# A fourth seven-product pair in each FFN of a two-layer encoder, with outputs added in a seeded PSUM bank

## The chip, the cores and the metric

The kernel runs on one core of a Trainium2 chip. The metric is the device time of one execution in microseconds (us), the median of several runs. The core has TensorE (matrix products; PE in the profile, with its weight loads as PEld), VectorE (DVE), ScalarE (ACT), GpSimd (POOL) and SyncE (SP, which here issues the loads of weights from memory). Each engine works through its own queue in order and waits on semaphores for what the others make. Matrix products are added up in PSUM, in banks of 128 x 512 fp32 values; everything else stands in SBUF.

## The reference

A two-layer encoder over 256 tokens of width 1024, in fp32. Each layer has two branches (gated linear attention and grouped-query attention), two gates that merge them, a SwiGLU feed-forward network (FFN) and an embedding that is added at the end. The change lies in the FFN and in gate B.

```python
D_MODEL, SEQ, DEPTH = 1024, 256, 2
FFN_HIDDEN = -(-8 * D_MODEL // (3 * 256)) * 256      # 2816 = 11 blocks of 256

def hybrid_layer(h, ...):
    u = rms_norm(h, g_mix_pre)
    (..., gate_a, gate_b) = jnp.split(u @ w_in, offsets, axis=-1)
    ...
    mixed = jax.nn.sigmoid(gate_a) * branch_a + jax.nn.sigmoid(gate_b) * branch_b
    h = h + rms_norm(mixed @ w_out, g_mix_post)

    gate, up = jnp.split(rms_norm(h, g_ffn_pre) @ w_ffn_in, 2, axis=-1)
    h = h + rms_norm((jax.nn.silu(gate) * up) @ w_ffn_out, g_ffn_post)

    e = p_i @ w_ple_proj
    return h + rms_norm(jax.nn.sigmoid(h @ w_ple_gate) * e, g_ple_post)
```

## The kernel before

**Products.** The 256 tokens are two halves of 128. Every fp32 operand is kept as a high and a low part in a reduced format (fp32r), and a product is three passes: high by high, low by high, high by low. Weights come in *units* of 128 x 2048 values, 1 MB, which is four slices of 128 rows by 512 columns. One unit against one half of the tokens is 12 matmuls of 128 x 512 (`passes`, L112): first the eight that need the unit's high part `wh`, then the four that need its low part `wl`. Against both halves a unit is 24 matmuls.

**The stream of weights** (`Stream`, L245). A plan, written out once for all layers, lists the units in order. SyncE loads a unit into one of two `raw` tiles. `split` (L130) then makes its parts, each in two pieces of 1024 columns: ScalarE copies the high part (L132), VectorE subtracts it from the source for the low part (L133; `vsub`, L128, is the line that the profile shows). The parts go to one of four `wh`/`wl` pairs of the pool `wp`. The stream runs ahead of TensorE as far as these tiles allow.

**Pairs of blocks with seven products** (`seven`, L608). Two column blocks of 512 by two halves of the contraction form a 2 x 2 matrix of units b11, b12, b21, b22; the tokens' two halves by the two halves of the contraction form another, a11 to a22. Instead of eight products of 12 matmuls, seven are made of sums of the a's and sums of the b's. The token sums are made by VectorE and split once per FFN (`sums`, L583; the four *forms*). The sums of units are made by `Stream.step` (L320), one call per product, with in-place adds of 2048 columns on VectorE. In its code the pair's four loads are x (b11), z (b12), y (b22) and q (b21): x and z are loaded into one of the `wp` pairs that the stream lends for this (`lent`, L275; the next pair's x and z may not be loaded before `lend` is set in the last step), y into a `big` tile, and q into a `raw` tile. The seven outputs are combined to four output blocks by 512-column operations on VectorE (L615 and `vsub`), with copies of single products from PSUM to SBUF by ScalarE (L635, L638, L642). For a pair of FFN blocks, the output blocks are gate and up of one token half each, and `gated` (L1438) makes SiLU(gate) on ScalarE and multiplies by up on VectorE.

**The FFN's order.** The hidden width is 11 blocks of 256. Blocks 0 and 1 come first, by halves. Then a string written by hand (L40) sets the order: `u` is a plain unit (24 matmuls; two make a block), a digit is that product of the current pair (12 matmuls), `o` is one step of the output projection (24 matmuls with a unit of `w_ffn_out`), `p` a load of a gain. Before each output step, the hidden values it needs are turned by TensorE transposes and split (hidden parts, tile `hid`, via `turned`, L1382). Blocks 4, 5 and 10 are plain, and 2-3, 6-7 and 8-9 are pairs.

```python
FFN = "uu12u34u5u67" "uo12o34o5o67" "poo12o345o67"
PLAIN, PAIRS = (4, 5, 10), (2, 6, 8)
OUT = (0, 1, 2, 3, 4, 5, 10, 6, 7, 8, 9)
```

Gate B is one more such pair, with plain units between its products (`GATES`, L47: `uuu1u2m34m5m67m`). The order of instructions within each engine's queue comes from a scheduler that works by priorities over this program order, so that an operation can stand earlier in a queue than its line suggests.

## Time and profile before

| what | before |
|---|---|
| time, median of 3 runs (range) | 924.27 us (923.92 to 924.66) |
| profiled execution, span from its first to its last instruction | 922.9 us |
| mean granted TensorE clock | 0.998 |
| TensorE matmuls busy | 912.2 us, 99% of the span |
| VectorE busy | 786.1 us, 85% |
| ScalarE busy | 578.5 us, 63% |
| bytes read from memory | 169.50 MB, 187 GB/s with what is written |

Busy times of neighbouring instructions of an engine overlap a little, so what one instruction costs its queue is read from the start of one to the start of the next. The profile names tiles without their numbers: `acc_0ffnin` is any accumulator of layer 0's FFN input, `wl_1ffnin` any low part in layer 1's. L numbers are lines of the kernel; helpers such as `vsub` (L128) and `vmul` (L125) give one line to many operations, which are told apart by their tiles.

### The profile page before, as it was taken

The page shows a single profiled execution, that of the slowest core. Times are in us where ns is not written, and L with a number is a line of the kernel's source. Part 1 is how long each engine was busy: PE and PEld are TensorE (multiplying, and loading weights), DVE is VectorE, ACT ScalarE, POOL GpSimd, SP SyncE. Part 2 cuts the span into 40 slices and gives each one's busy share as a digit, 9 for nine tenths or more (in the row PEclk, how much of TensorE's full clock was granted, in tenths as well). Part 3 has the DMA queues.
Part 4 walks back from the last instruction along what each step waited for, and adds up shares of the span by engine and source line. Part 5 has one row for each costly group of instructions (what it writes and reads, how often), then busy time and mean ns, then how long its engine had stood idle before and what let it go on. Part 6 is the DMA issues. An engine that isn't in the chain of part 4 may idle for free.

```text
span 922.9 us, 12406 instructions
## 1 busy us (share of the span) xinstructions
PE 912.2 (99%) x4668; PEld 776.2 (84%) x4668; DVE 786.1 (85%) x1002; ACT 578.5 (63%) x954; POOL 83.8 (9%) x147
## 2 busy tenths in 40 slices
PE   9999999999999999999999999999999999999996
PEld 6898888888888888888899988888888888888885
DVE  6898989987579998999779789798875799989884
ACT  4669676664567656566676677765644766565563
POOL 3400211300000000000114001100001000000000
PEclk9999999999999999999999999999999999999999
DMA  7463455656286565647576424454573756545361
GB/s 260 144 230 134 148 173 188 201 193 232 90 277 222 178 233 168 265 128 268 188 256 220 153 92 137 137 191 174 195 260 104 268 177 204 223 177 217 126 239 45
DMA packets 88679, 173.44 MB, mean 188 GB/s; under 512 B 3422, under 2 KB 26470, under 8 KB 88108
## 3 DMA queue, kind: packets, MB, share of 16 engines
q1 hardware_dynamic: 88460, 172.40, 54.0%
q8 instruction: 36, 0.59, 0.3%
q10 hardware_dynamic: 160, 0.27, 0.1%
q14 instruction: 23, 0.19, 0.1%
HBM read 169.50 MB, written 3.15 MB: 187 GB/s over the span
## 4 chain that ended last, share of the span: by engine, by line
PE 94%; DVE 2%; ACT 1%; DMA 1%; issue 1%; POOL 0%; POOLq 0%; DVEq 0%; ACTq 0%; SPq 0%
PE acc_0ffnin L120 12%; PE acc_1ffnin L120 11%; PE acc_1gate L120 7%; PE acc_0gate L120 7%; PE acc_0ffnin L104 7%; PE acc_1ffnin L104 7%; PE acc_1rq L120 3%; PE acc_0gqk L120 2%; PE acc_0wout L120 2%; PE acc_1gqk L120 2%; PE acc_1ple L120 2%; PE acc_0ple L120 2%; PE acc_0gg L120 2%; PE acc_1gg L120 2%; PE acc_0v L120 2%; PE acc_1merge L120 2%
## 5 line engine op out<-in xcount | busy, mean ns | idle before, releaser
L104 PE MATMUL acc_0ffnin<-wh_0ffnin,big_0ffnin 128*128 128x512 f32 x176 | 56.9, 393 | 0.0
L104 PE MATMUL acc_1ffnin<-wh_1ffnin,big_1ffnin 128*128 128x512 f32 x176 | 56.8, 392 | 0.0
L132 ACT CAST wh_1ffnin<-raw_1ffnin 128x1024 fp32r<-128x1024 f32 x38 | 38.5, 1049 | 27.3 <-DMA raw_1ffnin<-in_w_ffn_out_dram 8.7
L132 ACT CAST wh_0ffnin<-raw_0ffnin 128x1024 fp32r<-128x1024 f32 x38 | 38.4, 1048 | 23.8 <-PE acc_0ffnin L120 7.8
L128 DVE TENSOR_TENSOR wl_1ffnin<-raw_1ffnin,wh_1ffnin 128x1024 fp32r<-128x1024 f32 x38 | 45.0, 1221 | 8.9 <-ACT wh_1ffnin L132 8.9
L128 DVE TENSOR_TENSOR wl_0ffnin<-raw_0ffnin,wh_0ffnin 128x1024 fp32r<-128x1024 f32 x38 | 44.8, 1220 | 7.1 <-ACT wh_0ffnin L132 7.0
L120 PE MATMUL acc_1ffnin<-wh_1ffnin,big_1wout 128*128 128x512 f32 x168 | 42.5, 393 | 0.0
L120 PE MATMUL acc_0ffnin<-wh_0ffnin,big_0wout 128*128 128x512 f32 x168 | 42.5, 393 | 0.0
L104 PEld LDWEIGHTS acc_0ffnin<-wh_0ffnin,big_0ffnin 128*128 128x128 f32 x176 | 33.0, 188 | 7.1 <-DVE big_0ffnin L128 0.5
L104 PEld LDWEIGHTS acc_1ffnin<-wh_1ffnin,big_1ffnin 128*128 128x128 f32 x176 | 33.1, 188 | 6.7
L128 DVE TENSOR_TENSOR wl_1ffnin<-lent_1ffnin,wh_1ffnin 128x1024 fp32r<-128x1024 f32 x30 | 35.8, 1218 | 1.7 <-ACT wh_1ffnin L132 1.7
L128 DVE TENSOR_TENSOR wl_0ffnin<-lent_0ffnin,wh_0ffnin 128x1024 fp32r<-128x1024 f32 x30 | 35.8, 1216 | 1.7 <-ACT wh_0ffnin L132 1.7
L120 PEld LDWEIGHTS acc_1ffnin<-wh_1ffnin,big_1wout 128*128 128x128 f32 x168 | 31.1, 188 | 6.2
L120 PEld LDWEIGHTS acc_0ffnin<-wh_0ffnin,big_0wout 128*128 128x128 f32 x168 | 31.1, 188 | 6.2
L132 ACT CAST wh_1ffnin<-lent_1ffnin 128x1024 fp32r<-128x1024 f32 x30 | 30.7, 1053 | 7.1 <-PE acc_1ffnin L104 3.9
L132 ACT CAST wh_0ffnin<-lent_0ffnin 128x1024 fp32r<-128x1024 f32 x30 | 30.7, 1054 | 6.7 <-PE acc_0ffnin L104 3.9
L104 PE MATMUL acc_0ffnin<-wl_0ffnin,big_0ffnin 128*128 128x512 f32 x88 | 34.3, 389 | 0.0
L104 PE MATMUL acc_1ffnin<-wl_1ffnin,big_1ffnin 128*128 128x512 f32 x88 | 34.3, 389 | 0.0
L128 DVE TENSOR_TENSOR wl_1gate<-raw_1gate,wh_1gate 128x1024 fp32r<-128x1024 f32 x20 | 23.6, 1219 | 5.4 <-ACT wh_1gate L132 5.3
L128 DVE TENSOR_TENSOR wl_0gate<-raw_0gate,wh_0gate 128x1024 fp32r<-128x1024 f32 x20 | 23.7, 1226 | 4.8 <-ACT wh_0gate L132 4.8
L132 ACT CAST wh_0gate<-raw_0gate 128x1024 fp32r<-128x1024 f32 x20 | 20.0, 1048 | 11.7 <-DMA raw_0gate<-in_w_o_attn_dram 5.6
L132 ACT CAST wh_1gate<-raw_1gate 128x1024 fp32r<-128x1024 f32 x20 | 20.0, 1049 | 11.5 <-DMA raw_1gate<-in_w_o_attn_dram 5.5
(695 smaller groups left out, 2691.8 us busy)
## 6 DMA issues: line engine op xcount, KB each, us to landing
raw_0ffnin<-in_w_ffn_out_dram SPq DMA_DIRECT2D x11, 1024.0 KB, 6.6
raw_1ffnin<-in_w_ffn_out_dram SPq DMA_DIRECT2D x11, 1024.0 KB, 5.1
lent_0ffnin<-in_w_ffn_in_dram SPq DMA_DIRECT2D x6, 1024.0 KB, 7.4
lent_1ffnin<-in_w_ffn_in_dram SPq DMA_DIRECT2D x6, 1024.0 KB, 8.3
raw_0v<-in_w_in_dram SPq DMA_DIRECT2D x4, 1024.0 KB, 4.9
raw_0gate<-in_w_o_gla_dram SPq DMA_DIRECT2D x4, 1024.0 KB, 4.9
raw_0gate<-in_w_o_attn_dram SPq DMA_DIRECT2D x4, 1024.0 KB, 5.1
raw_0wout<-in_w_ffn_in_dram SPq DMA_DIRECT2D x8, 512.0 KB, 4.9
```

What stands on the lines that cost most here:

```text
L104: return nc.tensor.matmul(o, lhsT, rhs, start=start, stop=stop)
L120: nc.tensor.matmul(o, x, y, start=start and n == 0, stop=stop and n == len(seq) - 1, **kw)
L128: nc.vector.tensor_tensor(out=out, in0=in0, in1=in1, op=ALU.subtract)
L132: nc.scalar.copy(hi, src)
```

## The change

- Blocks 4 and 5 become a fourth pair (4-5), block 10 stays plain. The string is new: products 1 to 4 of a pair follow one another, then an output step, then 5, 6 and 7.
- `step` makes the unit sums in another order: product 2 now uses x+z, product 3 the unit q, product 4 the sum with y, product 5 y, product 6 the sum with q, product 7 the sum z+y. q is loaded before product 3 and not before 5; lending is allowed, and loading started, in step 6 and no longer in 7.
- One PSUM bank is held for a whole stage (`bank`: the first accumulator of the stage). VectorE seeds it with p5 − p1 after product 2; product 4 adds onto it; ScalarE copies it out to u4; product 5 adds onto it, ScalarE copies it out as c12 and writes u4 back into it; product 7 adds onto that, and it serves as the last output block. Two 512-column VectorE operations per pair are left beside the SiLU multiplies, where there were five.
- Low parts of the pairs' units (gate B's too), of the output units and of plain block 10 are made by one VectorE subtract of 2048 columns. High parts are still copied in two pieces of 1024.

```diff
-FFN = "uu12u34u5u67" "uo12o34o5o67" "poo12o345o67"
-PLAIN, PAIRS = (4, 5, 10), (2, 6, 8)
-OUT = (0, 1, 2, 3, 4, 5, 10, 6, 7, 8, 9)
+FFN = "uu1234o567" "oo1234o567" "po1234o567" "o1234o567"
+PLAIN, PAIRS = (10,), (2, 4, 6, 8)
+OUT = (0, 1, 10, 2, 3, 4, 5, 6, 7, 8, 9)
...
-                    if n == 5:
+                    if n == 3:
                         self.loads.append(q)
...
         def made(self, x):
-            for piece in self.put(x):
-                split(*piece)
+            pieces = self.put(x)
+            if not x.wide:
+                for piece in pieces:
+                    split(*piece)
+                return
+            for hi, _, src in pieces:
+                nc.scalar.copy(hi, src)
+            wh, wl = (t[:, : x.n] for t in self.ready[-1])
+            vsub(wl, x.raw[:, : x.n], wh.bitcast(F32))
 
         def step(self, n, x, y, z, q):
-            c = slice(0, 2048)
+            def add(to, b):
+                c = slice(0, 2048)
+                nc.vector.tensor_tensor(out=to.raw[:, c], in0=to.raw[:, c], in1=b.raw[:, c], op=ALU.add)
+
             if n == 1:
                 self.made(x)
-                nc.vector.tensor_tensor(out=x.raw[:, c], in0=x.raw[:, c], in1=z.raw[:, c], op=ALU.add)
+                add(x, z)
             elif n == 2:
+                self.made(x)
+                add(x, y)
+            elif n == 3:
+                self.made(q)
+            elif n == 4:
+                self.made(x)
+                add(x, q)
+                self.load()
+            elif n == 5:
                 self.made(y)
-                nc.vector.tensor_tensor(out=z.raw[:, c], in0=z.raw[:, c], in1=y.raw[:, c], op=ALU.add)
-            elif n == 3:
-                self.made(x)
-                nc.vector.tensor_tensor(out=x.raw[:, c], in0=x.raw[:, c], in1=y.raw[:, c], op=ALU.add)
-            elif n == 4:
-                self.made(z)
-            elif n == 5:
-                self.made(x)
-                nc.vector.tensor_tensor(out=x.raw[:, c], in0=x.raw[:, c], in1=q.raw[:, c], op=ALU.add)
+                add(z, y)
             elif n == 6:
-                self.made(q)
-            else:
-                self.load()
                 self.made(x)
                 self.held -= 1
                 self.lend = True
+                self.start()
+            else:
+                self.made(z)
...
-    def seven(sp, forms, gated):
+    def seven(sp, forms, gated, bank):
...
+        (p1, u4), (c12, c21) = (halves(mid()) for _ in range(2))
+        c11, p5 = acc(), acc()
+
+        def upper():
+            nc.scalar.copy(c12, bank[0])
+            nc.scalar.copy(bank[0], u4)
+            gated(0, c11, c12)
 
         def last():
-            vsub(v, p5, c22)
-            gated(1, v, c22)
+            vsub(c21, p1, bank[0])
+            gated(1, c21, bank[0])
 
         times(c11, quad(0, 0), True, lambda: nc.scalar.copy(p1, c11))
         yield
         task.need()
-        product(0, lambda: nc.scalar.copy(p3, o[0]))
+        times(p5, form(1), True, lambda: vsub(bank[0], p5, p1))
         yield
-        times(p5, form(1), True, lambda: vsub(v, p5, p1))
+        times(c11, quad(0, 1), False)
         yield
-        product(2, lambda: nc.scalar.copy(p7, o[0]))
+        times(bank[0], form(3), False, lambda: nc.scalar.copy(u4, bank[0]))
         yield
-        product(3, both)
+        times(bank[0], form(0), False, upper)
         yield
-        times(c11, quad(0, 1), False, lambda: gated(0, c11, c12))
+        times(p5, quad(1, 1), False, lambda: nc.scalar.copy(p1, p5))
         yield
-        times(p5, quad(1, 1), False, last)
+        times(bank[0], form(2), False, last)
         yield
...
+                if not hf + b:
+                    bank = [o]
```

28 lines of the change are left out of this document (13 added, 15 removed).

## The prediction, made before the changed kernel ran

> **What bounds the kernel now.** I read the page first: the sums by engine and the chain that ended last.
>
> ```profile
> span 922.9 us, 12406 instructions
> PE 912.2 (99%) x4668; PEld 776.2 (84%) x4668; DVE 786.1 (85%) x1002; ACT 578.5 (63%) x954; POOL 83.8 (9%) x147
> PEclk9999999999999999999999999999999999999999
> PE 94%; DVE 2%; ACT 1%; DMA 1%; issue 1%; POOL 0%; POOLq 0%; DVEq 0%; ACTq 0%; SPq 0%
> ```
>
> TensorE makes the end: 94% of the chain. Its waits, in the view of waits for that engine, are all of the list:
>
> ```profile
> PE warm L104 <- DVE keep L142: 1.6, 1, 1.6
> PE acc_0rq L120 <- ACT big_start L142: 0.6, 1, 0.6
> PE aux_start L142 <- DVE mid_start L142: 0.4, 1, 0.4
> PE aux_1at L104 <- DVE mid_1at L128: 0.2, 1, 0.2
> ```
>
> That is 2.8 us, and none of it in the FFN. So a matmul less is worth its whole price, as long as the other engines keep up; and any microsecond that they fall behind is added at full price too. VectorE's 85% over the span hides where it works. The windows of the pair stretch in layer 0 (columns: stretch, length, then busy time of PE, PEld, DVE, ACT, POOL, the granted clock, DMA share, GB/s) show it:
>
> ```profile
> 283.00:296.00 13.00, 13.00 (x61) 10.71 (x60) 13.00 (x14) 8.38 (x14) 0.00 (x0) 1.00 0.64 210
> 296.00:320.00 24.00, 24.00 (x110) 19.87 (x109) 22.66 (x22) 15.95 (x20) 0.00 (x0) 1.00 0.39 133
> 320.00:343.00 23.00, 23.00 (x107) 19.07 (x106) 22.32 (x24) 12.28 (x16) 0.95 (x1) 1.00 0.75 274
> 343.00:369.00 26.00, 26.00 (x120) 21.53 (x120) 22.83 (x20) 17.61 (x21) 0.00 (x0) 1.00 0.45 147
> 369.00:391.00 22.00, 22.00 (x101) 18.21 (x100) 20.53 (x20) 10.52 (x13) 0.00 (x0) 1.00 0.74 280
> 391.00:421.00 30.00, 30.00 (x136) 24.85 (x135) 27.56 (x26) 20.78 (x24) 0.00 (x0) 1.00 0.43 132
> ```
>
> From 283 to 421 us TensorE is busy all 138.0 us and VectorE 128.9: 93%, and 13.00 of 13.00 in the first stretch. This is the engine to which the change gives more work. (ScalarE has 85.5 of 138.)
>
> **The change part by part.** Prices first, start to start, since busy times of neighbours overlap.
>
> ```profile
> 282.26 1.88 DVE L128 TENSOR_TENSOR mid_0ffnin<-mid_0wout,mid_0ffnin 128x512 fp32r<-128x512 f32 x3
> 284.06 1.22 DVE L128 TENSOR_TENSOR wl_0ffnin<-raw_0emb,wh_0ffnin 128x1024 fp32r<-128x1024 f32 x1
> ...
> 285.53 0.41 DVE L125 TENSOR_TENSOR t_0ffnin<-acc_0ffnin,t_0ffnin 128x256 f32<-128x256 f32 x1
> 285.87 1.21 DVE L128 TENSOR_TENSOR wl_0ffnin<-raw_0emb,wh_0ffnin 128x1024 fp32r<-128x1024 f32 x1
> 287.00 2.35 DVE L128 TENSOR_TENSOR wl_0ffnin<-lent_0ffnin,wh_0ffnin 128x1024 fp32r<-128x1024 f32 x2
> 289.27 0.68 DVE L128 TENSOR_TENSOR mid_0ffnin<-t_0ffnin,mid_0ffnin 128x512 fp32r<-128x512 f32 x1
> 289.87 2.28 DVE L324 TENSOR_TENSOR lent_0ffnin<-lent_0ffnin,lent_0ffnin 128x2048 f32<-128x2048 f32 x1
> 292.07 0.41 DVE L128 TENSOR_TENSOR big_0ffnin<-aux_0ffnin,big_0ffnin 128x256 fp32r<-128x256 f32 x1
> ```
>
> VectorE: 512 columns (284.06 − 282.26)/3 = 0.60; 256 columns 285.87 − 285.53 = 0.34; a low part in two 1024 pieces 289.27 − 287.00 = 2.27; an add of 2048 columns 292.07 − 289.87 = 2.20. A low part 2048 wide isn't in this trace: I give it the add's 2.20, same width and sources; bounds 2.20 and the 2.28 that the row has as busy.
>
> ```profile
> 284.19 5.46 PE acc_0ffnin L120 x24
> 289.65 0.22 PE aux_0ffnin L439 x2
> ```
>
> TensorE, from the chain of waits: a matmul 5.46/24 = 0.2275, a transpose 0.11.
>
> *Removed.* Two blocks cost 96 matmuls as plain units, 84 as a pair: 12 fewer per FFN, 24 in all, the very count of that row: −5.5 us.
>
> *Moved to VectorE.* Per FFN the fourth pair brings four adds of 2048 columns, 8.8 us, and three units more to split (7 against 4), 6.6. Off go 1.8 per pair for the output sums (five 512 operations become two), some 0.07 per unit for wide splits, and the plain blocks' multiplies. What decides is where this falls. In the new order of products, 1 2 3 4 run with nothing between them, and at most an output step between 7 and the next 1. VectorE works its queue in order, and the bank's seed (`bank = p5 − p1`) is new: product 4 adds to the bank, so TensorE waits there. By the changed program's queue, ahead of the seed stand the low parts of 1, 2, 3, 4, the adds x+z, z+y, x+y, x+q, and the small operations between.
>
> *First pair.* Here VectorE has no slack and TensorE's time of product 1 is as before:
>
> ```profile
> 295.18 1.98 PE L120 MATMUL acc_0ffnin<-wh_0ffnin,big_0wout 128*128 128x512 f32 x8
> ...
> 300.62 1.98 PE L120 MATMUL acc_0ffnin<-wh_0ffnin,big_0wout 128*128 128x512 f32 x8
> 302.43 1.07 PE L120 MATMUL acc_0ffnin<-wl_0ffnin,big_0wout 128*128 128x512 f32 x4
> 303.35 0.60 PE L1424 MATMUL aux_0ffnin<-ident,t_0ffnin 128*128 128x128 f32 x4
> ```
>
> Before, plain block 4's second unit had its low part done at 287.0. One wide subtract can't be cut around the SiLU multiply between its halves, 0.5 later: 287.5. Then low part 1 2.2, a form 0.6, hidden part 0.34, x+z 2.2 (292.8), multiply 0.34, z+y 2.2, low 2 2.2 (297.6), multiply 0.34, x+y 2.2, low 3 2.2 (302.3, just in time for 302.43), low 4 2.2, hidden 0.6, x+q 2.2, seed 0.6: 307.9. TensorE ends product 3 at 303.35, then four transposes (0.44) and four high matmuls of the output step that stand ahead of product 4 (0.91): ready at 304.7. **Stall 3.2 us.**
>
> *Between pairs* the same loop closes on itself. The next pair's x lands in the buffer whose last reader is low part 6, so its load can't be issued before that. From one seed: x+q, output step, 5, 6, four operations of 2048 columns, 8.8 us; then the load, whose price is in these rows of SyncE's queue and ScalarE:
>
> ```profile
> 373.87 0.92 SPq L294 DMA_DIRECT2D lent_0ffnin<-in_w_ffn_in_dram  x2
> 379.07 2.01 ACT L132 CAST wh_0ffnin<-lent_0ffnin 128x1024 fp32r<-128x1024 f32 x2 [0.90 <-DMA lent_0ffnin<-in_w_ffn_in_dram]
> ```
>
> ScalarE waited for x, so it landed 379.07 − 373.87 = 5.2 us after issue. Here VectorE does low 7, low of an output step and a multiply (5.0) and then idles. ScalarE's two copies of 512 columns stand ahead of the cast, 1.2 by the row
>
> ```profile
> 298.20 0.58 ACT L635 COPY mid_0ffnin<-acc_0ffnin 128x512 f32<-128x512 f32 x1
> ```
>
> (a copy into PSUM is not in the trace: 0.5 to VectorE's 0.7), the cast 2.0 as above: 8.8 + 5.2 + 1.2 + 2.0 = 17.2. Then seven operations of 2048 columns (low 1, 2, 3, 4, x+z, z+y, x+y), 15.4, and five small ones of 0.6, 3.0, to the next seed: 35.6, with 0.2 for hand-overs (0.2 is the longest late wait of TensorE above) 35.8. TensorE's work in that loop, with one output step (24 matmuls) beside seven products (84) and a second output step (24): 132 × 0.2275 + 8 × 0.11 = 30.9. **Stall 4.9 us**, before pairs 3 and 4. Between pairs 1 and 2 stand two output steps, then TensorE has 24 matmuls more, 36.4 against 35.8: no stall (up to 0.6 to spare, lost if VectorE's operations cost 2.28).
>
> Landing is bounded by 4.9 below (other 1 MB loads) and 6.6 above:
>
> ```profile
> raw_0ffnin<-in_w_ffn_out_dram SPq DMA_DIRECT2D x11, 1024.0 KB, 6.6
> raw_0v<-in_w_in_dram SPq DMA_DIRECT2D x4, 1024.0 KB, 4.9
> ```
>
> *At nothing:* wide low parts in the gate and output stages and the gate pair's bank (units lie between its products, as now, which give VectorE some 5 us each; without them it would stall like the FFN); 12 casts and 26 copies more on ScalarE, in its 38% idle, except the 1.2 above; q's load moved earlier in SyncE's queue, behind raw loads that are waiting anyway. z's load waits for TensorE and is needed one add after x, no later than the x chain.
>
> *Sum:* per layer 3.2 + 0 + 4.9 + 4.9 = 13.0, twice 26.0, less 5.5: +20.5. On the span 922.9 that is 943.4; the median lies 1.4 above that span (924.27), so **945 us**, some 2.2% slower. Its own range: with the first pair's stall hidden after all, 945 − 6.4 = 938.6; with operations at 2.28 (11 on each loop's path, 0.9) and landing 6.6 (1.4) in four loops, and 0.7 (9 operations) for each first pair, 945 + 10.6 = 955.6.
>
> **The rivals.** (a) *The saving lands whole.* For it: VectorE's sums rise by little over the whole span, and TensorE never waited for it so far. Against it: from product 1 to product 4 TensorE needs 9.5 us (295.18 to 304.7), and VectorE's queue from low 1 to the seed 18.4; no lead covers that where VectorE already ran 13.00 of 13.00. 924.3 − 5.5 = 918.8. Chance 0.09. (b) *VectorE's own work is the only limit*: if x lands and is cast before VectorE has come to it, the loop is 8.8 + 5.0 + 18.4 = 32.2 and the later stalls 1.3 each: 2 × (3.2 + 1.3 + 1.3) = 11.6 − 5.5, +6.1: 930.4. Against it: it needs the load issued 3.4 us ahead of low part 6, and that buffer is in use. If still more is hidden it comes near no change. Chance 0.08, of which 0.03 for no change. (c) *A restart costs more.* The first matmuls of the kernel:
>
> ```profile
> 1.65 3.17 PE L104 MATMUL warm<-keep 128*128 128x512 bf16 x7 [1.65 <-DVE keep L142]
> ```
>
> Seven in 3.17 us, 0.45 each, twice the 0.2275 of later, though the clock row shows a full clock there. If TensorE starts so again after each stall, 3.17 us at half pace lose 7 × 0.2275 = 1.6 us; six stalls, 9.6: 955. Against it: the clock row shows no such stretch, but no wait here after the start is over 0.6 us. Chance 0.07. The Trainium skill, "TensorE: Matmul & The Clock Gate", Part 1: The HAM clock gate, has a rule for it: the array falls to half rate after an idle window of about 3.4 us and is back after as much sustained work. By that rule stalls of 4.9 us would always pay and those of 3.2 mostly not, four of six, which would give some 951; the start agrees with it (0.45 against 0.2275), the rest no row here shows.
>
> **How the numbers follow.** Forecast 0.76, (a) 0.09, (b) 0.08, (c) 0.07. About 0.2%, 1.8 us, is what this kernel's measurement can tell from no change. Faster: (a), 0.09. Same: 0.03, of (b). Slower: 0.05 + 0.76 + 0.07 = 0.88. The range reaches from 928, below (b)'s 930.4, to 958, above the forecast's 955.6 and most of (c); (a) and the rest of (b) are left out, with some of (c).
>
> **What would show it.** TensorE's waits, now 2.8 us, would be some 29, with the bank's seed on VectorE as releaser ahead of product 4 in the first, third and fourth pair of both FFNs, about 3, 5 and 5 us, and nothing in the second. 24 fewer 512-column matmuls; wide low parts near 2.28 busy. VectorE without a gap from block 10 to the first seed, with one gap of about 3 us in later pairs while x lands, ended by ScalarE's cast. The step on the load is wrong if VectorE has no such gap, the seed step if TensorE waits for low parts or for nothing. A time under 926 with no new waits is (a); matmuls at 0.45 after a stall are (c).

## The result and the profile after

The changed kernel takes 964.0 us (median of 4 runs, 962.94 to 964.17) against 924.38 of the kernel before on the same chip (923.92 to 924.66): a ratio of 1.0422, 95% interval 1.0409 to 1.0434. That is 39.6 us slower. The forecast had the sign and the places of the waits in the FFN, but 20.7 us, and its range ended at 958. One execution of a version below, order_wide, took 5203.52 us, far above its other three, and its ratio leaves it out.

First the page of the changed kernel: its span, the sums by engine, the granted clock in 40 slices, and the chain that ended last.

```profile
span 962.3 us, 12308 instructions
PE 921.2 (96%) x4644; PEld 776.8 (81%) x4644; DVE 798.1 (83%) x902; ACT 600.7 (62%) x988; POOL 80.0 (8%) x147
PEclk9999999999999999999899999999999999999999
PE 76%; DVE 15%; ACT 4%; issue 3%; DMA 1%; POOL 0%; SPq 0%; POOLq 0%; DVEq 0%; ACTq 0%
```

The matmuls fell by the 24 of the change (4668 to 4644), but TensorE's share of the last chain fell from 94% to 76%: VectorE and ScalarE now stand in it. One slice of the clock row shows an 8, where before all were 9. The view of TensorE's waits (line waited for, releaser, total, times, longest), first rows:

```profile
PE aux_0ffnout L457 <- DVE h L555: 7.4, 1, 7.4
PE acc_0ffnin L120 <- DVE wl_0ffnin L128: 6.1, 2, 3.0
PE acc_1ffnin L120 <- DVE wl_1ffnin L128: 6.1, 2, 3.1
PE acc_1ffnin L120 <- DVE acc_1ffnin L128: 4.2, 2, 3.4
PE acc_0ffnin L120 <- DVE acc_0ffnin L128: 3.4, 1, 3.4
```

Per FFN there is one wait of 3.4 us for the bank's seed (pair 1; in layer 1 a short one besides) and two of 3.0 for a low part (pairs 3 and 4). The largest wait of all, 7.4, is at the end of layer 0 and in no line of the forecast.

**Pair 1.** TensorE's timeline, then VectorE's (start, duration, instruction, idle time before and its releaser):

```profile
304.11 1.08 PE L104 MATMUL acc_0ffnin<-wh_0ffnin,big_0ffnin 128*128 128x512 f32 x4
308.63 3.48 PE L120 MATMUL acc_0ffnin<-wh_0ffnin,mid_0ffnin 128*128 128x512 f32 x8 [3.43 <-DVE acc_0ffnin L128]
```

```profile
305.68 2.28 DVE L337 TENSOR_TENSOR lent_0ffnin<-lent_0ffnin,raw_0ffnin 128x2048 f32<-128x2048 f32 x1
307.88 0.69 DVE L128 TENSOR_TENSOR acc_0ffnin<-acc_0ffnin,mid_0ffnin 128x512 f32<-128x512 f32 x1
```

The seed starts at 307.88 and x+q, 2.20 ahead of it, as the forecast's queue had it. New is what follows the wait: eight matmuls in 3.48 us, 0.43 each, where 0.2275 is usual. Product 4 of this pair costs some 1.5 us more.

**From pair to pair.** Product 4 starts at 308.63, 346.47, 383.18 and 419.17 in layer 0:

```profile
346.47 2.01 PE L120 MATMUL acc_0ffnin<-wh_0ffnin,mid_0ffnin 128*128 128x512 f32 x8
...
379.72 1.95 PE L120 MATMUL acc_0ffnin<-wl_0ffnin,big_0wout 128*128 128x512 f32 x4 [3.05 <-DVE wl_0ffnin L128]
...
419.17 2.88 PE L120 MATMUL acc_0ffnin<-wh_0ffnin,mid_0ffnin 128*128 128x512 f32 x8
```

The loops are 37.84, 36.71 and 35.99. TensorE's own work in them, by the forecast's count, is 36.4, 30.9 and 30.9, so 1.4, 5.8 and 5.1 are lost. VectorE's timeline in the second of these loops, then ScalarE's, TensorE's and SyncE's rows beside its gap:

```profile
345.65 0.69 DVE L128 TENSOR_TENSOR acc_0ffnin<-acc_0ffnin,mid_0ffnin 128x512 f32<-128x512 f32 x1
...
358.11 2.29 DVE L128 TENSOR_TENSOR wl_0ffnin<-lent_0ffnin,wh_0ffnin 128x2048 fp32r<-128x2048 f32 x1 [2.97 <-PE acc_0ffnin L120]
360.31 0.69 DVE L125 TENSOR_TENSOR t_0ffnin<-mid_0ffnin,t_0ffnin 128x512 f32<-128x512 f32 x1
360.92 2.29 DVE L128 TENSOR_TENSOR wl_0ffnin<-raw_0ffnin,wh_0ffnin 128x2048 fp32r<-128x2048 f32 x1
363.32 2.29 DVE L128 TENSOR_TENSOR wl_0ffnin<-lent_0ffnin,wh_0ffnin 128x2048 fp32r<-128x2048 f32 x1
...
381.78 0.69 DVE L128 TENSOR_TENSOR acc_0ffnin<-acc_0ffnin,mid_0ffnin 128x512 f32<-128x512 f32 x1
```

```profile
356.01 2.00 ACT L330 CAST wh_0ffnin<-lent_0ffnin 128x1024 fp32r<-128x1024 f32 x2 [4.89 <-PE acc_0ffnin L104]
...
361.29 2.00 ACT L330 CAST wh_0ffnin<-lent_0ffnin 128x1024 fp32r<-128x1024 f32 x2
```

```profile
355.58 0.39 PE L104 MATMUL acc_0ffnin<-wh_0ffnin,big_0ffnin 128*128 128x512 f32 x1
...
356.94 1.07 PE L120 MATMUL acc_0ffnin<-wl_0ffnin,mid_0ffnin 128*128 128x512 f32 x4
```

```profile
355.16 0.98 SPq L298 DMA_DIRECT2D lent_0ffnin<-in_w_ffn_in_dram  x2
```

VectorE's operations of 2048 columns are 2.28 busy and 2.20 from start to start, as forecast. Its gap of 2.97 us is there too, but two units earlier than forecast: ahead of low part 7 (358.11), not ahead of the next pair's low part 1 (363.32). ScalarE's cast for product 7 (356.01) had waited 4.89 us for TensorE at line 104, which is the output step behind product 4: its last matmul ends at 355.97, and that frees a weight buffer. VectorE's own row names another releaser, TensorE at line 120: these are product 5's low matmuls, which end at 358.01, just when the cast does. So product 7 seems to wait for two buffers, one for its high part, that the output step frees, and one for its low part, that product 5 frees behind it. In pair 1 the second alone ends the gap: there the cast is done at 319.61, product 5's low matmuls end at 320.29, and low part 7 starts at 320.38. The cast of the next pair's x at 361.29 shows no wait; ScalarE comes to it from other work 6.1 us after SyncE issued the load.

**The end of layer 0.** Where the next layer's decay weights are loaded and split, and the FFN's post norm; before (SyncE, VectorE):

```profile
396.12 0.31 SPq L717 DMA_DIRECT2D mid_0ffnin<-in_w_alpha_up_dram  x1
```

```profile
419.84 1.22 DVE L128 TENSOR_TENSOR mid_0ffnin<-mid_0ffnin,mid_0ffnin 17x1024 fp32r<-17x1024 f32 x1
...
431.70 1.28 DVE L125 TENSOR_TENSOR mid_0ffnout<-acc_0ffnin,mid_0ffnin 128x512 f32<-128x512 f32 x2
```

and after (SyncE, GpSimd, VectorE, TensorE):

```profile
447.55 0.50 SPq L729 DMA_DIRECT2D mid_0ffnin<-in_w_alpha_up_dram  x1
```

```profile
449.36 0.57 POOL L511 TENSOR_TENSOR rstd_0ffnout<-rstd_0ffnout,neghalf 128x1 f32<-128x1 f32 x1
```

```profile
455.29 2.36 DVE L128 TENSOR_TENSOR wl_0ffnout<-raw_0ffnin,wh_0ffnout 128x1024 fp32r<-128x1024 f32 x2 [2.79 <-ACT wh_0ffnout L132]
457.68 1.22 DVE L128 TENSOR_TENSOR mid_0ffnin<-mid_0ffnin,mid_0ffnin 17x1024 fp32r<-17x1024 f32 x1
458.91 1.29 DVE L125 TENSOR_TENSOR mid_0ffnout<-acc_0ffnin,mid_0ffnin 128x512 f32<-128x512 f32 x2
```

```profile
460.91 1.97 PE L457 MATMUL aux_0ffnout<-ident,h 128*128 128x128 f32 x8 [7.42 <-DVE h L555]
```

Before, the last of the three small loads of weights left SyncE's queue at 396.12, and the split (17 x 1024) ran 12 us ahead of the post norm. Now that load leaves at 447.55, behind raw loads which wait for buffers; the split runs at 457.68, and the post norm of the first half, whose statistics were ready at 449.9, stands behind it and behind low parts that wait for their casts. TensorE waits 7.4 us for `h` and then runs at half rate again (eight small transposes in 1.97 us). The windows view has a granted clock of 0.91 there (columns as in the prediction):

```profile
430.00:470.00 40.00, 32.58 (x145) 26.69 (x144) 29.68 (x29) 22.33 (x32) 1.73 (x4) 0.91 0.65 226
```

**The ledger.** For every matmul of a stage I took the time from its start to the next start, less the median of matmuls of its size, and summed. The FFN of layer 0 has 17.4 us of such excess more than before, that of layer 1 17.6, the end of layer 0 10.0. With the 24 matmuls less, 17.4 + 17.6 + 10.0 − 5.5 = 39.5; the spans differ by 962.3 − 922.9 = 39.4. Layer 0's 17.4 is 3.6 at pair 1's seed, 1.4, 5.8 and 5.1 in the loops, and 1.5 behind pair 4.

### The profile page after: what moved, and what is told of

Read it like the earlier page. It is cut to its first block, busy times and chain, and to the rows that moved or that the text cites. A ratio compares the mean times of both kernels' runs of the same rounds, so it can differ in the third digit from the quotient of the medians.

```text
span 962.3 us, 12308 instructions
## 1 busy us (share of the span) xinstructions
PE 921.2 (96%) x4644; PEld 776.8 (81%) x4644; DVE 798.1 (83%) x902; ACT 600.7 (62%) x988; POOL 80.0 (8%) x147
## 4 chain that ended last, share of the span: by engine, by line
PE 76%; DVE 15%; ACT 4%; issue 3%; DMA 1%; POOL 0%; SPq 0%; POOLq 0%; DVEq 0%; ACTq 0%
PE acc_0ffnin L120 7%; PE acc_1gate L120 7%; PE acc_0gate L120 7%; PE acc_1ffnin L120 5%; PE acc_0ffnin L104 5%; PE acc_1ffnin L104 5%; DVE wl_1ffnin L128 3%; DVE wl_0ffnin L128 3%; DVE lent_1ffnin L337 3%; PE acc_0ple L120 2%; PE acc_1rq L120 2%; PE acc_0gqk L120 2%; DVE lent_0ffnin L337 2%; PE acc_0wout L120 2%; PE acc_1gqk L120 2%
## 5 line engine op out<-in xcount | busy, mean ns | idle before, releaser
L330 ACT CAST wh_1ffnin<-lent_1ffnin 128x1024 fp32r<-128x1024 f32 x40 | 40.4, 1051 | 36.4 <-DVE lent_1ffnin L337 13.5
L330 ACT CAST wh_0ffnin<-lent_0ffnin 128x1024 fp32r<-128x1024 f32 x40 | 40.5, 1052 | 36.3 <-PE acc_0ffnin L104 12.7
L128 DVE TENSOR_TENSOR wl_1ffnin<-lent_1ffnin,wh_1ffnin 128x2048 fp32r<-128x2048 f32 x20 | 45.7, 2287 | 14.1 <-PE acc_1ffnin L120 9.9
L128 DVE TENSOR_TENSOR wl_0ffnin<-lent_0ffnin,wh_0ffnin 128x2048 fp32r<-128x2048 f32 x20 | 45.7, 2287 | 13.9 <-PE acc_0ffnin L120 9.8
L120 PE MATMUL acc_1ffnin<-wh_1ffnin,mid_1ffnin 128*128 128x512 f32 x128 | 35.1, 414 | 4.3 <-DVE acc_1ffnin L128 4.2
L120 PE MATMUL acc_0ffnin<-wh_0ffnin,mid_0ffnin 128*128 128x512 f32 x128 | 35.2, 415 | 3.4 <-DVE acc_0ffnin L128 3.4
L128 DVE TENSOR_TENSOR wl_0ffnin<-raw_0ffnin,wh_0ffnin 128x2048 fp32r<-128x2048 f32 (+1 forms) x17 | 36.5, 2160 | 2.0 <-ACT wh_0ffnin L330 1.6
L128 DVE TENSOR_TENSOR wl_1ffnin<-raw_1ffnin,wh_1ffnin 128x2048 fp32r<-128x2048 f32 (+1 forms) x17 | 36.5, 2158 | 1.6 <-ACT wh_1ffnin L330 1.6
L120 PEld LDWEIGHTS acc_1ffnin<-wh_1ffnin,mid_1ffnin 128*128 128x128 f32 x128 | 24.8, 199 | 11.8 <-DVE acc_1ffnin L128 5.5
L120 PEld LDWEIGHTS acc_0ffnin<-wh_0ffnin,mid_0ffnin 128*128 128x128 f32 x128 | 25.4, 203 | 10.8 <-DVE acc_0ffnin L128 4.7
L128 DVE TENSOR_TENSOR wl_0gate<-raw_0gate,wh_0gate 128x1024 fp32r<-128x1024 f32 (+1 forms) x19 | 24.3, 1319 | 5.4 <-ACT wh_0gate L132 5.2
```

The source lines that it names most:

```text
L120: nc.tensor.matmul(o, x, y, start=start and n == 0, stop=stop and n == len(seq) - 1, **kw)
L128: nc.vector.tensor_tensor(out=out, in0=in0, in1=in1, op=ALU.subtract)
L330: nc.scalar.copy(hi, src)
```

## The experiments

All were timed in 3 rounds beside the kernel before on the same chip. Ratios are to that kernel. Its medians on the chips used are 924.4 to 925.3 us, so a difference of 1 us between two versions says little.

### The end of layer 0

**late_up.** The small loads and the split moved behind the post norms.

```diff
-        if l + 1 < DEPTH:
-            wup_next = up_weights(l + 1)
...
+        if l + 1 < DEPTH:
+            wup_next = up_weights(l + 1)
         e = big().rearrange("p (s c) -> p s c", s=2)
         nc.sync.dma_start(e, kept)
```

> The changed kernel, with the loading and splitting of the next layer's decay weights moved behind the FFN's post norms. Theory: the 7.4 us wait at the end of layer 0's FFN comes from that split, which stands ahead of the post norm in VectorE's queue and waits for its third small load; without it the wait and the half-rate matmuls after it go, about 10 us: 953 to 956 us. Rival: VectorE is late there because the whole FFN left it late; then the wait stays within 2 us and the time with it, 961 to 964.

Measured: 964.89 (963.0 to 967.13), ratio 1.0429 (1.0411 to 1.0447). Nothing gained. The wait of 7.4 is gone, but another load now comes late:

```profile
PE aux_1emb L869 <- DMA mid_0ffnout<-in_p_dram: 4.5, 1, 4.5
```

The load of `p` stands behind the small loads in SyncE's queue. The wait moved with the loads, so this place of the edit couldn't price it.

**up_at_gain.** The same lines moved ahead instead: to the load of the post norm's gain, before pair 3.

```diff
                 gpost = gain(a["g_ffn_post"][l], mid(), D)
+                if l + 1 < DEPTH:
+                    wup_next = up_weights(l + 1)
...
-        if l + 1 < DEPTH:
-            wup_next = up_weights(l + 1)
```

> The changed kernel, with the loads and the split of the next layer's decay weights put at the load of the FFN's post-norm gain, ahead of pair 3. Theory: the 10 us at the end of layer 0 come from small loads that stand between unit loads which wait for their buffers in SyncE's queue, and from work queued behind them on VectorE; moved this far ahead they are out of the way both there and for the embedding's load: 951 to 956 us, with no wait over 1 us between the FFN and the embedding gate. Rival: the end is late because the FFN leaves the queues late, whatever stands there; then the wait finds a third place and the time stays 960 to 965.

Measured: 954.6 (953.23 to 955.98), ratio 1.0318 (1.0298 to 1.0338). As expected: 9.4 us less than the changed kernel, so that much of the loss is the end of layer 0. What is left of its wait, and what the move costs in pair 3 of layer 0 (ScalarE's copy of the decay weights delays a copy that TensorE waits for):

```profile
PE acc_0ffnin L120 <- ACT mid_0ffnin L647: 4.8, 1, 4.8
...
PE aux_0ffnout L457 <- DVE h L555: 0.4, 1, 0.4
```

Most of the further runs start from this version, 954.6.

### Which part of the change

**old_string.** The changed kernel with the plan of before: three pairs, units between the products.

```diff
-FFN = "uu1234o567" "oo1234o567" "po1234o567" "o1234o567"
-PLAIN, PAIRS = (10,), (2, 4, 6, 8)
-OUT = (0, 1, 10, 2, 3, 4, 5, 6, 7, 8, 9)
+FFN = "uu12u34u5u67" "uo12o34o5o67" "poo12o345o67"
+PLAIN, PAIRS = (4, 5, 10), (2, 6, 8)
+OUT = (0, 1, 2, 3, 4, 5, 10, 6, 7, 8, 9)
```

> The changed kernel with the order of products, plain blocks and output steps of before (three pairs, units between the products); the new products with the bank, the wide low parts and the earlier load of q stay. No matmul is saved. If the cost of the change lies in products 1 to 4 standing with nothing between them, the bank's seed is always made in time here and nothing waits: 922 to 929. If the bank or the wide low parts cost by themselves wherever they stand (half of what is left after the end of layer 0, some 15): 935 or more.

Measured: 931.58 (930.84 to 933.12), ratio 1.0077 (1.006 to 1.0094), between the two. The trace tells what the time does not: no wait above 0.2 us is left in either FFN; the one new wait is again at the end of layer 0.

```profile
PE aux_0ffnout L457 <- DVE h L555: 4.1, 1, 4.1
```

In the ledger the end of layer 0 has 6.9 us more than before, the FFN of layer 1 0.7, and the spans differ by 6.2 (929.1 − 922.9). Bank, wide low parts and the new order of unit sums cost TensorE nothing in the FFN where other units stand between the products; what they cost here is the late end of layer 0.

**order_only.** The reverse: the kernel before with the new plan alone, its own products and narrow low parts.

```diff
-FFN = "uu12u34u5u67" "uo12o34o5o67" "poo12o345o67"
-PLAIN, PAIRS = (4, 5, 10), (2, 6, 8)
-OUT = (0, 1, 2, 3, 4, 5, 10, 6, 7, 8, 9)
+FFN = "uu1234o567" "oo1234o567" "po1234o567" "o1234o567"
+PLAIN, PAIRS = (10,), (2, 4, 6, 8)
+OUT = (0, 1, 10, 2, 3, 4, 5, 6, 7, 8, 9)
```

> The kernel before with the new string, four pairs and the new order of output units alone: old output sums, old unit sums, low parts in two pieces. Theory: the new spacing of the products is the cause, and bank and wide low parts only soften it: 955 to 975 us, with TensorE waiting for low parts in every pair. Rival: the seed of the bank is the cause; then without it TensorE doesn't wait and the time is 919 to 928.

Measured: 942.44 (941.82 to 945.89), ratio 1.0198 (1.0177 to 1.0218), between the two again. The fourth pair with its plan costs 17 us net without any bank. The windows from the add x+z of pair 1 to that of pair 4 in layer 1, three loops, first of this kernel, then of the changed one:

```profile
750.65:862.35 111.70, 107.31 (x480) 87.42 (x479) 108.38 (x99) 67.57 (x81) 0.00 (x0) 1.00 0.53 194
```

```profile
768.31:880.09 111.78, 104.70 (x451) 84.18 (x450) 99.14 (x60) 68.12 (x83) 0.00 (x0) 0.97 0.52 183
```

Here VectorE is busy 108.4 of 111.7 us: its own work nearly fills the stretch. In the changed kernel it is busy only 99.1, and the three loops take the same time. The bank and the wide parts took work off VectorE, as they should, and the loops got no shorter: there VectorE's gaps, not its work, are what counts. What the changed kernel takes more, some 22 us, is 10.0 at the end of layer 0 and, by the ledger, 6.6 and 5.5 in the two FFNs, nearly all outside these loops.

At the end of layer 0 TensorE doesn't wait for `h` in this run, and the last load of the next layer's decay weights leaves SyncE's queue as early as in the kernel before; in old_string it leaves later. First this run, then old_string:

```profile
395.12 0.31 SPq L717 DMA_DIRECT2D mid_0ffnin<-in_w_alpha_up_dram  x1
```

```profile
421.10 0.33 SPq L729 DMA_DIRECT2D mid_0ffnin<-in_w_alpha_up_dram  x1
```

So it is not the new string that makes these loads late. It is not the wide low parts either: order_wide has them, and there the load leaves at 397.10.

**order_wide.** order_only with low parts of 2048 columns.

```diff
-            for piece in self.put(x):
-                split(*piece)
+            pieces = self.put(x)
...
+            wh, wl = (t[:, : x.n] for t in self.ready[-1])
+            vsub(wl, x.raw[:, : x.n], wh.bitcast(F32))
```

> The kernel before with the new string and four pairs (as in order_only), and low parts of pairs, output units and block 10 made 2048 wide; still no bank. Theory: the bank, by its seed and the new order of unit sums, is what the changed kernel pays for beyond the string; wide low parts are neutral: 938 to 946 us, near order_only's 942. Rival: wide low parts cost, since they wait for both casts and can't be cut around small operations: 950 us or more.

Measured: 948.91, ratio 1.0255 (1.0236 to 1.0275): 6.5 more than order_only, between the two cases and nearer the rival. In the window of the same three loops VectorE is busy 107.97 of 113.60 us: the same work as in order_only, with more idle time. That this comes of wide parts not being taken in halves is likely, but not shown.

**narrow_up.** up_at_gain with narrow low parts, the bank kept.

```diff
-            self.wide = make in wide
+            self.wide = False
```

> The version with the decay weights loaded ahead of pair 3 (954.6), with low parts in two 1024-column pieces again; the bank stays. If the loop from seed to seed is the sum of VectorE's operations and the load, narrow parts change it by 0.07 an operation at most: 953 to 958. If it is the coarse grain of wide parts that costs, as between the two runs without the bank (948.91 and 942.44): 946 to 950.

Measured: 955.15 (954.2 to 957.56), ratio 1.033 (1.0314 to 1.0346): nothing against 954.6, as expected. With the bank the width of the low parts doesn't show in the time.

### Half rate after a wait

**fill_wait.** 12 matmuls of zeros into the bank of product 3, where TensorE waits, in pairs 1, 3 and 4. They add nothing to the sums.

```diff
+    def dummies(o, n):
+        for _ in range(n):
+            nc.tensor.matmul(o, zero, keep, start=False, stop=True, skip_group_check=True)
...
-        times(c11, quad(0, 1), False)
+        times(c11, quad(0, 1), False, pad=fill)
+        if not fill:
+            dummies(c11, first)
```

> The changed kernel with 12 matmuls of zeros, 2.7 us, put where TensorE waits in pairs 1, 3 and 4 (they add zero to product 3's bank). Theory: half-rate matmuls follow because TensorE stood idle; with the wait filled they go, VectorE's times stay, and 1.6 to 2 us are won at each of six places: 951 to 955 us. Rival: the slow matmuls come from something else (the bank that VectorE has just written, say) and stay, or the filling only delays: 961 to 980.

Measured: 959.52, ratio 1.0371 (1.0355 to 1.0386): 4.5 less than the changed kernel, where 9 to 13 were expected. Product 4 of pair 1, after the filled wait:

```profile
307.99 2.11 PE L121 MATMUL acc_0ffnin<-wh_0ffnin,mid_0ffnin 128*128 128x512 f32 x8 [0.83 <-DVE acc_0ffnin L131]
```

2.11 for eight, against 3.48: full rate. So the half rate follows from TensorE's idling and not from the data or the bank. From seed to seed the loops are now 36.38, 36.10 and 36.10 in both layers, against 37.77, 36.13 and 36.65. The first loop gets its 1.4 back; the later ones hardly change, because another chain sets them.

### What closes the loop of 36 us

**add_late.** z+y, which product 7 needs, pinned behind low part 6 and out of the way of the seed.

```diff
                 self.made(y)
-                add(z, y)
             elif n == 6:
-                self.made(x)
+                low = self.made(x)
+                with tc.issue_after(low.ins):
+                    add(z, y)
```

> The changed kernel, with the add z+y pinned behind product 6's low part. Theory: what stands ahead of the seed and of low part 3 in VectorE's queue sets TensorE's wait; 2.2 us less of it takes the first pair's wait from 3.4 to under 1 and those of pairs 3 and 4 from 3.0 to 1 to 2.5, and short waits leave no half-rate matmuls: 945 to 956 us. Rival: the load of the next pair's x is what sets the loop; then pairs 3 and 4 keep their 3 us and only the first pair's wait falls, 953 to 956, with the gap of VectorE growing by 2.

Measured: 968.38, ratio 1.0468 (1.0452 to 1.0483). Missed. Pair 1's wait shrank to 0.5, but the adds that make product 4's unit moved behind other low parts, and new waits for its cast came:

```profile
PE acc_0ffnin L120 <- ACT wh_0ffnin L330: 4.4, 2, 2.2
```

**x_early.** In up_at_gain, products 5 and 6 change places, so that x's buffer is free, and the next x loaded, one product earlier; the output step stands behind the new product 5.

```diff
-FFN = "uu1234o567" "oo1234o567" "po1234o567" "o1234o567"
+FFN = "uu12345o67" "oo12345o67" "po12345o67" "o12345o67"
...
             elif n == 5:
-                self.made(y)
-                add(z, y)
-            elif n == 6:
                 self.made(x)
                 self.held -= 1
                 self.lend = True
                 self.start()
+            elif n == 6:
+                self.made(y)
+                add(z, y)
...
```

> The changed kernel with products 5 and 6 exchanged, the output step moved behind the new product 5, lending one step earlier, and the decay weights at the gain as in up_at_gain. Theory: the loop between pairs is low part of x, load of the next x, cast, sums; with x's last low part two operations of 2048 columns earlier the loop falls from 36 us to VectorE's own 32 to 33, against TensorE's 30.9: waits of 1 to 2.5 us in place of 5 to 6, four times: 934 to 944 us. Rival: VectorE's queue and not the load sets the loop; then it stays near 36 and the time at 950 to 956.

Measured: 974.21, ratio 1.0531 (1.051 to 1.0551). Missed by 30 us: the product that needs the sum x+q now stands right behind product 4, and add, cast and low part follow one another with VectorE idle between (8.7 us for casts in layer 0's pairs; it waits 9.7 more there for TensorE's line 104). The exchange, and the earlier lending with it, is what costs: o_after5, below, has the same string without them. The seed comes late four times in each layer:

```profile
PE acc_0ffnin L120 <- DVE acc_0ffnin L128: 9.4, 4, 4.5
```

**x_early_pool.** x_early with z+y on GpSimd.

```diff
-                add(z, y)
+                add(z, y, nc.gpsimd)
```

> x_early with the add z+y on GpSimd. Theory: VectorE's work in a loop falls by 2.2 to about 30 us, under TensorE's 30.9, and the waits go but for the first pair's: 918 to 930 us. Rival: GpSimd's add takes long, or holds VectorE up while it runs, and z's low part comes late: no better than x_early, 936 us or more.

Measured: 998.14, ratio 1.079 (1.0767 to 1.0812). Missed: it is worse than x_early, as the rival had it. GpSimd's add, and VectorE's low part beside it:

```profile
293.42 4.63 POOL L337 TENSOR_TENSOR lent_0ffnin<-lent_0ffnin,big_0ffnin 128x2048 f32<-128x2048 f32 x1 [29.89 <-DVE lent_0ffnin L337]
```

```profile
295.41 4.78 DVE L128 TENSOR_TENSOR wl_0ffnin<-lent_0ffnin,wh_0ffnin 128x2048 fp32r<-128x2048 f32 x1 [1.79 <-ACT wh_0ffnin L330]
```

The add takes 4.63 us where VectorE needs 2.28, and the VectorE operation that ran beside it took 4.78 in place of 2.28. It ended 2.15 us after the add. In all ten places of this run, gate B included, such a subtract ended 2.15 to 2.16 after the add: about its own length, as if it had stood still until the add was through. Moving the add away saved VectorE nothing.

**spread_up.** up_at_gain with the output step between products 2 and 3 of each pair, and one less between the pairs.

```diff
-FFN = "uu1234o567" "oo1234o567" "po1234o567" "o1234o567"
+FFN = "uu12o34o567" "o12o34o567" "p12o34o567" "12o34o567"
```

> The version with the decay weights loaded ahead of pair 3 (954.6), with an output step between products 2 and 3 of each pair in place of one between the pairs. If the loop of VectorE and x's load from seed to seed sets the end of each pair, the output step's 5.5 us of TensorE work only move from behind the seed to ahead of it: the first pair's wait of 3.4 goes, and comes back as a longer wait in pair 2: 951 to 957. If the waits are a matter of what TensorE has ahead of product 4, each pair wins: 938 to 946.

Measured: 969.94 (967.66 to 970.84), ratio 1.0482 (1.0467 to 1.0498), outside both. The seed's wait is gone, but TensorE now waits for casts:

```profile
PE acc_0ffnin L120 <- ACT wh_0ffnin L330: 5.4, 2, 2.7
```

The loops of layer 0 grew to 41.6, 39.5 and 38.6. That an output step in that place holds a weight buffer while products 3 and 4 need theirs made is possible, but the waits don't show it: ScalarE's casts wait 9.0 us for the output steps in layer 0's pairs, against 10.3 in up_at_gain.

**x_stays.** up_at_gain, in which pairs 2 to 4 go on with the first pair's x buffer. x's load is left out in them.

```diff
+                        if b11 in stay:
+                            x.own = lambda: self.keep()
+                            x.stay = True
...
-                for dst, src in moves:
+                for dst, src in () if x.stay else moves:
```

> The version with the decay weights loaded ahead of pair 3 (954.6), in which pairs 2, 3 and 4 don't load x but go on with the first pair's buffer (its sum): x's load is left out, every other operation stays. If the load's issue and landing stand in the loop (6.1 us, of which VectorE has 5.0 us of other work and idles some 3.5 for load and cast), the loops to pairs 3 and 4 fall from 36 to some 32.5 and the time to 938 to 944. If VectorE's own work is the loop and the load is hidden: 951 to 956.

Measured: 951.59 (950.27 to 951.97), ratio 1.0285 (1.027 to 1.03): 3.0 less than 954.6, the case in which the load is hidden. VectorE's gap in the loop, and ScalarE's cast beside it, stand as they were, with no load to wait for:

```profile
359.74 2.29 DVE L128 TENSOR_TENSOR wl_0ffnin<-lent_0ffnin,wh_0ffnin 128x2048 fp32r<-128x2048 f32 x1 [2.93 <-PE acc_0ffnin L120]
```

```profile
357.64 2.00 ACT L343 CAST wh_0ffnin<-lent_0ffnin 128x1024 fp32r<-128x1024 f32 x2 [4.85 <-PE acc_0ffnin L104]
```

This overturned the forecast's loop. The gap is not x's landing; TensorE releases it, the cast by the output step and the low part by product 5. The loop to pair 3 did fall, in layer 1 from 36.1 to 33.2, but there the seed stands ahead of low part 4 in VectorE's queue, and the next loop is longer, 37.5: the two together are 1.5 us shorter.

**o_after5.** up_at_gain with the output step behind product 5.

```diff
-FFN = "uu1234o567" "oo1234o567" "po1234o567" "o1234o567"
+FFN = "uu12345o67" "oo12345o67" "po12345o67" "o12345o67"
```

> The version with the decay weights loaded ahead of pair 3 (954.6), with the output step inside each pair behind product 5 in place of ahead of it. New theory: the loop from seed to seed runs product 4 (2.7), the output step (5.5), whose end frees the weight buffer that product 7's cast waits for, the cast (2.0), then VectorE's queue without a gap. With the output step one product later, product 7's cast waits only for product 5: 2.7 less in each loop, four loops in the two layers: 942 to 948. If the loop isn't closed through that buffer: 952 or more.

Measured: 951.97 (950.11 to 954.24), ratio 1.0296 (1.0273 to 1.0319): 2.6 less, at the edge of "not closed through that buffer". The loops did fall, in layer 0 to 34.2 and 34.7 and in layer 1 to 32.8 and 35.8, but part came back behind pair 4. In this version low part 7 still starts only as the output step's low matmuls end, its releaser by the trace: it seems to get the buffer that the step's low part had. So the edit moved the release by less than I took it to.

**both_off.** x_stays and o_after5 together (x's load is left out in pairs 2 to 4; the diffs are those two).

> The version with the decay weights loaded ahead of pair 3 (954.6) with both suspects off together: pairs 2, 3 and 4 don't load x but go on with the first pair's buffer (x's load is left out), and the output step inside each pair stands behind product 5. If two chains of one length close the loop of 36 (x's load and cast; the output step that frees the buffer of product 7's cast), each alone won 3, and both together take the loops to VectorE's own 32.5: 3.5 less in each of four, less some 2 to 4 that come back behind pair 4: 940 to 945. If one of them is no part of it, the gain is that of the better one alone: 949 to 953.

Measured: 953.08 (951.34 to 954.6), ratio 1.0312 (1.0295 to 1.0329): the same as o_after5 alone within the ranges. Loops 34.2, 34.7, 33.1 and 35.8. On top of o_after5 x's load is worth nothing. The forecast that both chains gone would free 3.5 in each loop falls; of the two it is the buffer that holds.

**o_between.** up_at_gain with a pair's seven products in a row and its output steps between the pairs.

```diff
-FFN = "uu1234o567" "oo1234o567" "po1234o567" "o1234o567"
+FFN = "uu1234567" "ooo1234567" "poo1234567" "oo1234567"
```

> The version with the decay weights loaded ahead of pair 3 (954.6), with the seven products of a pair in a row and its output steps all between the pairs. By the theory of the weight buffers product 7's cast waits for product 4 alone, and the loop falls to VectorE's own 32.2: up to 3.8 less in each of four loops, 938 to 944. If the same limit comes back where two output steps stand ahead of the next pair (the buffers then hold these, and low parts 3 and 4 come late): 948 to 956. If a buffer has nothing to do with it: 953 to 956.

Measured: 975.68 (974.28 to 977.59), ratio 1.0548 (1.053 to 1.0566), worse than any of the three cases. The loops are 37.0 to 40.7. VectorE's low parts no longer wait for TensorE in layer 0's pairs, as the theory had it, but they now wait 12.7 us for casts (4.1 in up_at_gain), and casts 27.9 for VectorE's sums (14.0). I took the release ahead of product 7 for the only one; that two output steps in the buffers ahead of product 1 make the new waits is not shown.

**five_buffers.** up_at_gain with five buffers for high and low parts in place of four, and two big buffers fewer to make room.

```diff
-    wp = ctx.enter_context(tc.tile_pool(name="wp", bufs=4))
-    bigp = ctx.enter_context(tc.tile_pool(name="bigp", bufs=9))
+    wp = ctx.enter_context(tc.tile_pool(name="wp", bufs=5))
+    bigp = ctx.enter_context(tc.tile_pool(name="bigp", bufs=7))
...
-    ws = Stream(4)
+    ws = Stream(5)
```

> The version with the decay weights loaded ahead of pair 3 (954.6), with five buffers in place of four for the high and for the low parts of weights, and two big buffers fewer. By the theory of the weight buffers the cast of product 7 waits for product 4 and not for the output step behind it, and the loops fall from 36 towards VectorE's 32.2: 3.8 less in each of four, 938 to 945, if the two big buffers cost nothing outside the FFN; the loops tell it apart from that. The first pair's wait of 3.4 stays. If VectorE's queue alone sets the loop: loops of 36, 950 or more.

Measured: 943.53 (942.31 to 945.41), ratio 1.0201 (1.0185 to 1.0217): 11.1 less than 954.6, as expected in size. In layer 0's pairs VectorE's low parts waited 9.2 us for TensorE in up_at_gain; here none does. In layer 1 the seed's waits are down from 4.1 to 2.3 and the low parts' from 6.1 to 2.7:

```profile
PE acc_1ffnin L120 <- DVE wl_1ffnin L128: 2.7, 2, 1.4
PE acc_1ffnin L120 <- DVE acc_1ffnin L128: 2.3, 3, 0.8
```

Where the gain lies differs from what I wrote. The later loops fell by 1.1 each (36.10 to 34.99 in layer 1), not by 3.8. Most came from pair 1: its wait of 3.4 is gone in both layers, because VectorE could run one unit further ahead, and in layer 1 the half rate behind it (no wait there is over 1.4). Layer 0 has less of the gain: the wait that up_at_gain brought is 4.5 there, and one of 3.2 for the seed has come in pair 4. What still holds the loop at 35.0 is a buffer too, by the trace. ScalarE's cast for product 7, and VectorE's low part 7 behind it:

```profile
816.27 2.00 ACT L330 CAST wh_1ffnin<-lent_1ffnin 128x1024 fp32r<-128x1024 f32 x2 [4.06 <-DVE wl_1ffnin L128]
```

```profile
818.31 2.29 DVE L128 TENSOR_TENSOR wl_1ffnin<-lent_1ffnin,wh_1ffnin 128x2048 fp32r<-128x2048 f32 x1 [2.07 <-ACT wh_1ffnin L330]
```

The cast waits for VectorE's low part 6, whose end frees x's old buffer, and VectorE idles 2.07 for the cast.

No version here is faster than the kernel before. Of those with the fourth pair the best are order_only (942.4) and five_buffers (943.5); old_string, without it, takes 931.6.

## Why the prediction was wrong

**The saving** (−5.5): right, 24 matmuls fewer, and the stages outside the FFN and its end are unchanged to within some tenths.

**Pair 1** (3.2 per layer): right. The seed was forecast at 307.3 to 307.9 and started at 307.88; the wait is 3.43. **Pair 2** (none): right, no wait over 0.4 stands there.

**The loops** (35.8, 4.9 lost): right in size, wrong in mechanism. Seed to seed they are 36.13 and 36.65, and the losses 5.8 and 5.1; the TensorE wait stands at low part 3, just ahead of the seed. The first half of the sum (8.8 + 5.2 + 1.2 + 2.0 = 17.2 from the seed to low part 1) measures 363.32 − 345.65 = 17.67, but it is made of other parts: 0.82 from seed to product 4, 9.54 for product 4, a wait of 0.35, the first six matmuls of products 5 and 6 and the rest of the output step, 2.1 for the cast of product 7, 2.2 for its low part, 0.6 for a multiply, 2.4 for the output unit's low part. The second half, 18.4, measures 18.46. The step "and then idles", for x to land, is the one that failed here: x_stays took the load away and the gap stayed, and five_buffers took away VectorE's waits for TensorE and shrank the loop by 1.1. Two chains had nearly one length, and I priced the one I saw in the code: VectorE begins low part 1 at 363.32, only some 0.2 us after the work ahead of it, and x's cast had run until then (361.29 + 2.00). That the sum met the loop's length is thus partly luck.

**"At nothing", and the sum**: this is the step that made the number wrong. The list names the wide parts, the gate pair, ScalarE's casts, q's and z's loads, and it stops at the FFN's last pair. The next layer's decay weights were in no part of the change, but in the changed kernel their small loads stand behind raw loads that wait, and their split comes just ahead of the post norm. That is 10.0 us; up_at_gain took 9.4 of it away. Without it the time is inside the range: up_at_gain has 954.6. The string is not what moved the loads: order_only and order_wide have the new one and the loads at their old place, old_string has the old one and a wait of 4.1. What is left is the new order in `step`, with q's load ahead of product 3 and loading started in step 6, and the bank. The item of the list that comes nearest is "q's load moved earlier in SyncE's queue, behind raw loads that are waiting anyway", but no run tests it alone. The order of the queues at the FFN's end could have been compared as the seed's queue was.

**Rival (c)**, half rate after a stall (chance 0.07, 1.6 for each of six): the mechanism is real, the sum was not. Five of the six waits of 3.0 to 3.4 us are followed by seven to nine matmuls at 0.43, which is 1.4 to 1.8 us, as priced. But in pairs 3 and 4 this falls into a loop that VectorE and the buffers set anyway; it shows only in each first loop (1.4) and behind pair 4, and fill_wait won 4.5 of it. The Trainium skill, "TensorE: Matmul & The Clock Gate", Part 1: The HAM clock gate, gives some 3.4 us of idling for it. Here 3.0 was enough, and my reading of the page, that stalls of 3.2 would mostly not pay, was wrong. The page also calls the window free-running; the timeline ahead of pair 4's product 4 agrees in that the half rate doesn't start with the end of the wait:

```profile
416.36 1.20 PE L120 MATMUL acc_0ffnin<-wl_0ffnin,big_0wout 128*128 128x512 f32 x4 [3.05 <-DVE wl_0ffnin L128]
417.40 1.87 PE L104 MATMUL acc_0ffnin<-wh_0ffnin,big_0ffnin 128*128 128x512 f32 x4
```

After the wait four matmuls run at nearly full pace, and only then four in 1.87.

**Rival (b)**, VectorE's own work as the limit at 32.2: its size is right. The measured loop of 36.13 less VectorE's idle time in it (2.97 in the row shown, 0.56 for a cast of ScalarE, some 0.2 besides) is 32.4. No version held it; the shortest single loop is 32.82, in o_after5, and the one behind it is 35.80.

**The account.** Forecast +20.5 on the span, measured +39.4: 10.0 at the end of layer 0, and in each layer 0.4 in pair 1, 1.4 of half rate, 1.1 in the loops and 1.5 behind pair 4, 8.8 for two. Together 18.8.

What stays open: which part of the new `step` or the bank moved the small loads at the end of layer 0, which buffer releases would have to go to bring the loop to VectorE's 32.4 (a sixth buffer wasn't tried), and how much of five_buffers' gain is each of its two releases.

## What to carry to other kernels

When the order of work or of loads changes, compare every queue to the end of the layer, not only in the stage that was edited: a few small loads that slipped behind loads waiting for buffers cost here half as much as the whole forecast. A loop's sum that meets the measured time doesn't show the chain; ask of each gap who released it, and test with the supposed cause taken out. An engine that does less work can still cost time if its steps become serial, for how far it runs ahead is set by the number of buffers, and steps of other work between hold these too.

## What the runs showed of the hardware

A wait of TensorE of 3.0 us or more was mostly followed by 3 us or more at half rate: 0.43 per 512-column matmul against 0.2275. It isn't so each time: in the changed kernel one wait of 3.05 was not, and in up_at_gain one of 3.44 was not and another was followed by 14 such matmuls. In two versions a wait of 1.8 us was followed by it too (o_after5, both_off), while single waits of 1.4 were not (five_buffers). In fill_wait, where 12 matmuls of zeros filled the waits, no stretch at half rate followed them.

GpSimd's fp32 add of 128 x 2048 takes 4.63 us, twice VectorE's 2.28, and a VectorE subtract of that size beside it took 4.78; both figures recur in all eight FFN pairs of x_early_pool (4.60 to 4.63, and 4.78 to 4.95). The Trainium skill, "GPSIMD Engine Reference", 8. Key points, says that GpSimd shares its SBUF interfaces with VectorE and contends with its instructions that have two SBUF inputs; this pair of rows agrees.
